# A transformer layer on one core: the low part of the FFN weights made by ScalarE and an accumulating transfer instead of VectorE

## The chip, the cores and the metric

The kernel runs on one core of one Trainium2 chip. The core has TensorE (PE in the profile; the loading of its stationary operand is shown apart as PEld), VectorE (DVE), ScalarE (ACT), GpSimd (POOL) and SyncE (SP), and 16 DMA engines that they share for transfers between DRAM and the on-chip memory. The queues from which transfers are issued are written SPq, ACTq and POOLq. The metric is the device time of one execution in microseconds; before the change it is 1370.73 us (median of three runs, 1368.98 to 1370.79). A measurement of this kernel can tell a difference of about 0.2% from no change.

## The reference, cut to what matters

The program computes one layer of a bidirectional encoder on 256 tokens of 2048 features, all in float32:

```python
h = rms_norm(x, g_mix)
proj = h @ w_in                       # 2048 x 8256: latents, rotary key, dilated q/k/v, gates
...                                   # latent attention -> y_a, dilated attention -> y_b
x = x + (g[:, :, 0] * y_a + g[:, :, 1] * y_b) @ w_o
gt, up = jnp.split(rms_norm(x, g_ffn) @ w_gate_up, 2, axis=-1)   # 2048 x 11264
return x + (jax.nn.silu(gt) * up) @ w_down                       # 5632 x 2048
```

The last two lines are the FFN. The change touches only how the weights `w_gate_up` and `w_down` are prepared.

## The kernel before

**Products.** Every weight matrix is cut into groups of at most 512 columns, and each group into blocks of two times 128 rows ("chunks" in the code): a block is a tile of 128 partitions by 2 x 512 float32, 512 KB. There are 481 blocks in all, in one fixed order: `w_in` with the small projections in between, the two attention outputs, `w_o`, and then the FFN. The FFN has 176 blocks of `w_gate_up` and 88 of `w_down`, 264 together, and it is the last stage of the program.

**Two parts for each operand.** TensorE multiplies in the format float32r. To keep float32 precision each operand is split in a high part (the value rounded to float32r) and a low part (what the rounding left). A product is then three matmuls, `mm3` (lines 384 to 386): high by high (L384), low weight by high activation (L385), high weight by low activation (L386). A block has two row slices, two halves of the tokens and three matmuls for each: 12 matmuls. The first row slice's L384 needs the high part `wh` alone; the next matmul, L385, needs the low part `wl`.

**The way of a block.** `load(i)` issues the transfer of block i from DRAM into a tile `w` from SyncE (L702). `split(i)` lets ScalarE copy `w` into `wh` (L710; the copy rounds) and VectorE subtract, `wl = w - wh` (L711). `products(i)` issues the 12 matmuls. The tiles `w`, `wh` and `wl` have four buffers each (`AHEAD + 1`).

**The order.** The order on every engine is the order in which the program is written; nothing is rearranged. At step i of the main loop it is: load of block i+4, split of block i+3, products of block i, then what takes a finished group out of the accumulators, and one piece of side work. So `wh` and `wl` of block i+3 take the buffers of block i-1, and can be written once the products of block i-1 are done; the products of block i+3 come three blocks later. The load of block i+4 takes the `w` buffer of block i, and can start once that block has been split.

**Beside it.** In the FFN, ScalarE also computes the SiLU of each gate group (L596) and VectorE multiplies it with the up group (L604); the result is transposed on TensorE (L201) and split in the same way into `hid0`, `hid1` (L171, L176). GpSimd has almost nothing to do: the factors of the norms (L160, L162), and at the start seven transfers of gain vectors (L124). The last thing the program does is to add the last group to the residual (L626) and to store it.

Of the kernel before, what the change touches and what calls it, by code (L numbers as in the profile page):

```python
# [14 lines left out]
AF = mybir.ActivationFunctionType  # L15
ALU = mybir.AluOpType
# [3 lines left out]
P = 128  # L20
S = 256
NT = S // P
# [59 lines left out]
def layer_kernel(ctx: ExitStack, tc: tile.TileContext, a: dict, out: bass.AP):  # L82
    nc = tc.nc
# [17 lines left out]
    def f32(ap):  # L101
        return ap.bitcast(F32)
# [4 lines left out]

# [1 line left out]
    ident = small([P, P], "ident")  # L109
# [38 lines left out]
    gains = Job(job_gains())  # L148
# [15 lines left out]

# [1 line left out]
    def split_evac(*parts):  # L166
        """each part: hi, lo, source and a factor per partition; all hi first, since hi and lo of a part may share tiles
        with the next one's."""
        for hi, lo, ps, scale in parts:
            if scale is None:  # L170
                nc.scalar.copy(hi, ps)  # L171
            else:
                nc.scalar.activation(hi, ps, AF.Copy, scale=scale)  # L173
        for hi, lo, ps, scale in parts:
            if scale is None:
                nc.vector.tensor_sub(lo, ps, f32(hi))  # L176
            else:
                nc.vector.scalar_tensor_tensor(lo, ps, scale, f32(hi), op0=ALU.mult, op1=ALU.subtract)  # L178

    class Act:  # L180
        """hi and lo parts of a transposed activation, in tiles of 4 blocks."""

# [13 lines left out]
    def transpose_in(act, k0, nk, src, gname=None):  # L196
        """blocks k0..k0+nk (nk <= 4, in one tile of act) from src(t, k) [tok, 128]."""
        ps = side(f"tr_{act.name}{k0}").rearrange("p (k s) -> p k s", s=S)
        for k in range(nk):
            for t in range(NT):  # L200
                nc.tensor.transpose(ps[:, k, t * P:(t + 1) * P], src(t, k0 + k), ident)  # L201
        h, l = act.tiles(k0 // 4)
        o = k0 % 4
        if gname is None:
            split_evac((h[:, o:o + nk], l[:, o:o + nk], ps[:, :nk], None))
        else:
            split_evac(*((h[:, o + k], l[:, o + k], ps[:, k], gain(gname, k0 + k)) for k in range(nk)))
# [29 lines left out]

# [1 line left out]
    cT, latjob = {"cq": Act("cqT", 4), "ckv": Act("ckvT", 4)}, {}  # L239
# [20 lines left out]

# [1 line left out]
    pb = {}  # L262
# [35 lines left out]

# [1 line left out]
    mla = {}  # L300
# [39 lines left out]
    def rope(x, A, B, nh, i):  # L340
        """x [P, NT, nh, 64] rotated in place, with the gain in the tables."""
        c = rt[:, 2 * i, :, None, :].to_broadcast([P, NT, nh, ROPE])
        s = rt[:, 2 * i + 1, :, None, :].to_broadcast([P, NT, nh, ROPE])
        nc.vector.tensor_mul(A, x, c)
        nc.vector.tensor_mul(B, x, s)
        h = ROPE // 2
        nc.vector.tensor_sub(x[..., :h], A[..., :h], B[..., h:])
        nc.vector.tensor_add(x[..., h:], B[..., :h], A[..., h:])
# [30 lines left out]

# [1 line left out]
    oT = {"mla": Act("oaT", H), "dil": Act("obT", H)}  # L381
# [6 lines left out]
    def job_attn(kind, p):  # L388
        h0 = 2 * p
        nm = f"{kind}{p}"  # L390
        if kind == "mla":
            qk, aux = mla["qk", p], mla["r", p]
            ss, v, r = (small([P, 12], f"{nm}{c}") for c in ("ss", "vv", "rr"))
# [16 lines left out]
            q, k = ([qk[:, c, t] for t in range(NT)] for c in range(2))  # L410
            g, sc = gqk_mla, MLA_SCALE
            vh, vl = ([mla["v", p][:, c, t] for t in range(NT)] for c in range(2))
        else:
            q, k = ([z.rearrange("p (h d) -> p h d", h=H)[:, h0:h0 + 2] for z in pb[n]] for n in ("qd", "kd"))
            vh, vl = ([pb["vd"][t][c].rearrange("p (h d) -> p h d", h=H)[:, h0:h0 + 2] for t in range(NT)]
                      for c in range(2))
            g = gqk_dil
        # transposes of q and k
        ps = side(nm + "qk").rearrange("p (c h s) -> p c h s", c=2, h=2)
# [19 lines left out]
        yield 1  # L439
        # scores  # L440
        ps = side(nm + "s").rearrange("p (h t s) -> p h t s", h=2, t=NT)
# [9 lines left out]
        if kind == "mla":  # L451
            src, esc = sv, sc
# [15 lines left out]
        yield 2  # L468
        # transposes of the probabilities
        ps = side(nm + "pt").rearrange("p (h c s) -> p h c s", h=2, c=2)  # L470
# [6 lines left out]
        yield 2  # L477
        # values
        ps = side(nm + "o").rearrange("p (h s) -> p h s", s=S)
# [7 lines left out]
    def job_prep_dil(n):  # L487
        """the norms of all heads: keys are scaled, the queries' factor waits for the scores"""
        z = [t.rearrange("p (h d) -> p h d", h=H) for t in pb[n]]
        ss = small([P, NT, H], "ss_" + n)  # L490
        for t in range(NT):
            sq = t4([P, H, 128], f"sq_{n}{t}")
            nc.scalar.activation(sq, z[t], AF.Square)
            nc.vector.tensor_reduce(ss[:, t], sq, axis=AX.X, op=ALU.add)
            yield 1
        r = rstd_of(ss, 128, "r_" + n)
        yield 2
        if n == "qd":
            st["rqd"] = small([P, NT, H], "rqd")
            nc.vector.tensor_scalar_mul(st["rqd"], r, DIL_SCALE)  # L500
        else:
            for t in range(NT):
                nc.vector.tensor_mul(z[t], z[t], r[:, t, :, None].to_broadcast([P, H, 128]))
                yield 1
# [7 lines left out]

# [1 line left out]
    g0, tj, mT, gbias = {}, {}, Act("mT", KD), {}  # L514
# [44 lines left out]

# [1 line left out]
    x1, hT, hjobs, xres = {}, Act("hT", KD), {}, {}  # L561
# [26 lines left out]

# [1 line left out]
    sg, hidT, djobs = {}, {}, {}  # L590
# [37 lines left out]

# [1 line left out]
    groups = []  # L630
# [34 lines left out]
    for j in range(4):  # L665
        groups.append(Group(W["w_o"], 512 * j, 512, range(KD), mT, evac_wo(j),
                            {k: (lambda k=k: [mjobs[k // 4]]) for k in range(KD)}))
    halves = (range(0, 6), range(6, 11))
    for half, js in enumerate(halves):
# [22 lines left out]
    early = {}  # L692

    def load(i):
        g, gi, ks, _, _ = chunks[i]
        if gi == 0 and i:
            load_x(ks[0] * P, (ks[-1] + 1) * P)
            if ks[-1] == KD - 1:
                load_rows()
        t = wp.tile([P, len(ks), g.n], F32, name=f"w{i}", tag="w")  # L700
        src = g.w[ks[0] * P:(ks[-1] + 1) * P, g.c0:g.c0 + g.n]
        nc.sync.dma_start(t, src.rearrange("(k p) n -> p k n", p=P))  # L702
        wt[i] = t

    def split(i):
        g, gi, ks, _, _ = chunks[i]
        t = wt.pop(i)
        h = wp.tile([P, len(ks), g.n], F32R, name=f"wh{i}", tag="wh")
        l = wp.tile([P, len(ks), g.n], F32R, name=f"wl{i}", tag="wl")
        nc.scalar.copy(h, t)  # L710
        nc.vector.tensor_sub(l, t, f32(h))  # L711
        parts[i] = (h, l)
# [110 lines left out]
def _tables():  # L823
    """Rotary angles, distances and how many patterns reach a key: constants of the shapes."""
    f = np.float32
# [30 lines left out]
```

## Time and profile before

The times are 1370.79, 1368.98 and 1370.73 us. The profiled execution has a span of 1367.5 us from the first to the last instruction; the median of the times is 3.2 us above this span, and these 3.2 us are taken as what lies around the span, since the profiled execution has no separate time beside it.

| what | before |
|---|---|
| median time | 1370.73 us |
| span of the profiled execution | 1367.5 us |
| TensorE busy in the span | 1356.5 us (99%) |
| VectorE busy | 758.1 us (55%) |
| ScalarE busy | 623.5 us (46%) |
| GpSimd busy | 32.3 us (2%) |
| data moved | 257.14 MB, mean 188 GB/s |
| first FFN product starts | 634.42 us |

How to read it: the busy time of TensorE counts overlapping matmuls once, and a busy TensorE is not TensorE at its peak. A row of a group of instructions gives the line, the engine, the operation, the tile written and the tiles read, the shape, the count, the busy time in us and the mean duration of one in ns, and then the idle time of the engine just before them and what ended it. A row of a window gives the stretch in us, the busy time of each engine in it, the TensorE clock that was granted, the share of the 16 DMA engines' time that was busy with packets, and the data rate. A timeline row gives the start and the duration in us.

### The profile page before, as it was taken

Reading aid. Unit: us, or ns where it says so; the run is one execution under the profiler, and the core shown is the slowest. Engines: PE = TensorE matmul, PEld = TensorE weight load, DVE = VectorE, ACT = ScalarE, POOL = GpSimd, SP = SyncE. Lnnn points to the kernel's source line nnn. Section 1 sums busy time; section 2 is a strip of 40 time slices with the busy share of each in tenths; the row PEclk is TensorE's granted clock in tenths of the full one; section 3 lists DMA queues with packets and bytes.
Section 4 is the critical chain, followed back from the end, with each engine's and each line's share of the span. In section 5 each row is a group of like instructions: output and inputs, shape, how many; then the busy total and the mean of one; then the engine's idle time right before and its main releaser. Section 6 shows DMA issues by size and latency. Waiting matters only on the chain.

```text
span 1367.5 us, 16361 instructions
## 1 busy us (share of the span) xinstructions
PE 1356.5 (99%) x6342; PEld 1144.7 (84%) x6342; DVE 758.1 (55%) x774; ACT 623.5 (46%) x776; POOL 32.3 (2%) x41
## 2 busy tenths in 40 slices
PE   7999999999999999999999999999999999999998
PEld 6899999888888888888888888888888888888887
DVE  5566777677655556555445544554444544555443
ACT  6555655454444444445444444433344444444332
POOL 1011111000000000000000000000000000000000
PEclk9999999999999999999999999999999999999999
DMA  8555555555566666565665665555665665565663
GB/s 259 175 173 168 158 172 177 174 166 172 178 202 199 198 190 216 193 210 181 196 192 182 191 198 184 187 189 193 194 193 187 194 197 188 186 188 183 202 212 123
DMA packets 138205, 257.14 MB, mean 188 GB/s; under 512 B 9192, under 2 KB 28688, under 8 KB 138128
## 3 DMA queue, kind: packets, MB, share of 16 engines
q1 hardware_dynamic: 137760, 255.96, 59.8%
q8 instruction: 49, 0.80, 0.2%
q14 instruction: 28, 0.23, 0.0%
q10 hardware_dynamic: 144, 0.13, 0.0%
q0 software_dynamic: 224, 0.01, 0.0%
HBM read 253.97 MB, written 2.10 MB: 187 GB/s over the span
## 4 chain that ended last, share of the span: by engine, by line
PE 99%; DMA 1%; SPq 0%; DVE 0%; issue 0%; ACT 0%; DVEq 0%
PE g L384 31%; PE g L386 31%; PE g L385 31%; PE tr_hid L201 1%; DMA w<-in_w_in_dram 1%; PE tr_hT L201 0%; PE tr_mT L201 0%; PE tr_xT L201 0%; DMA xn<-in_x_dram 0%; PE mla3s L386 0%; PE mla2s L386 0%; PE mla0s L386 0%; PE mla1s L386 0%; PE mla2s L385 0%; PE mla2s L384 0%; PE mla1s L385 0%
## 5 line engine op out<-in xcount | busy, mean ns | idle before, releaser
L711 DVE TENSOR_TENSOR wl<-w,wh 128x1024 fp32r<-128x1024 f32 (+2 forms) x481 | 575.6, 1201 | 472.8 <-ACT wh L710 470.8
L710 ACT CAST wh<-w 128x1024 fp32r<-128x1024 f32 (+2 forms) x481 | 496.2, 1036 | 537.6 <-PE g L386 489.7
L384 PE MATMUL g<-wh,hTh 128*128 128x512 f32 x704 | 274.8, 390 | 0.0
L386 PE MATMUL g<-wh,hTl 128*128 128x512 f32 x704 | 274.0, 389 | 0.0
L385 PE MATMUL g<-wl,hTh 128*128 128x512 f32 x704 | 273.9, 389 | 0.0
L384 PE MATMUL g<-wh,xTh 128*128 128x512 f32 (+1 forms) x544 | 210.2, 386 | 1.9 <-ACT xTh L173 1.9
L386 PE MATMUL g<-wh,xTl 128*128 128x512 f32 (+1 forms) x544 | 207.2, 381 | 0.5 <-DVE xTl L178 0.5
L385 PE MATMUL g<-wl,xTh 128*128 128x512 f32 (+1 forms) x544 | 207.2, 381 | 0.0
L386 PEld LDWEIGHTS g<-wh,hTl 128*128 128x128 f32 x704 | 132.1, 188 | 27.6
L385 PEld LDWEIGHTS g<-wl,hTh 128*128 128x128 f32 x704 | 132.2, 188 | 27.1
L384 PEld LDWEIGHTS g<-wh,hTh 128*128 128x128 f32 x704 | 132.2, 188 | 27.1
L384 PEld LDWEIGHTS g<-wh,xTh 128*128 128x128 f32 x544 | 102.7, 189 | 17.2 <-ACT xTh L173 2.1
L386 PEld LDWEIGHTS g<-wh,xTl 128*128 128x128 f32 x544 | 102.4, 188 | 17.3 <-DVE xTl L178 1.0
L385 PEld LDWEIGHTS g<-wl,xTh 128*128 128x128 f32 x544 | 102.6, 189 | 15.3 <-DVE wl L711 0.4
L384 PE MATMUL g<-wh,hid0h 128*128 128x512 f32 x192 | 74.8, 390 | 0.0
L386 PE MATMUL g<-wh,hid0l 128*128 128x512 f32 x192 | 74.7, 389 | 0.0
L385 PE MATMUL g<-wl,hid0h 128*128 128x512 f32 x192 | 74.7, 389 | 0.0
L384 PE MATMUL g<-wh,hid1h 128*128 128x512 f32 x160 | 62.3, 390 | 0.0
L386 PE MATMUL g<-wh,hid1l 128*128 128x512 f32 x160 | 62.2, 389 | 0.0
L385 PE MATMUL g<-wl,hid1h 128*128 128x512 f32 x160 | 62.2, 389 | 0.0
L384 PE MATMUL g<-wh,mTh 128*128 128x512 f32 x128 | 50.2, 392 | 0.0
L386 PE MATMUL g<-wh,mTl 128*128 128x512 f32 x128 | 49.8, 389 | 0.0
(509 smaller groups left out, 1233.5 us busy)
## 6 DMA issues: line engine op xcount, KB each, us to landing
w<-in_w_gate_up_dram SPq DMA_DIRECT2D x176, 512.0 KB, 4.5
w<-in_w_down_dram SPq DMA_DIRECT2D x88, 512.0 KB, 4.3
w<-in_w_in_dram SPq DMA_DIRECT2D x79, 512.0 KB, 4.2
w<-in_w_in_dram SPq DMA_DIRECT2D x56, 448.0 KB, 3.6
w<-in_w_o_dram SPq DMA_DIRECT2D x32, 512.0 KB, 4.5
w<-in_w_o_mla_dram SPq DMA_DIRECT2D x16, 512.0 KB, 4.1
w<-in_w_o_dil_dram SPq DMA_DIRECT2D x16, 512.0 KB, 4.2
w<-in_w_ukv_dram SPq DMA_DIRECT2D x8, 512.0 KB, 4.3
```

The costliest lines, as they stand in the source:

```text
L201: nc.tensor.transpose(ps[:, k, t * P:(t + 1) * P], src(t, k0 + k), ident)
L384: nc.tensor.matmul(ps, ah, bh, start=first, stop=False)
L385: nc.tensor.matmul(ps, ah, bl, start=False, stop=False)
L386: nc.tensor.matmul(ps, al, bh, start=False, stop=last)
L710: nc.scalar.copy(h, t)
L711: nc.vector.tensor_sub(l, t, f32(h))
```

## The change

For the blocks of the FFN (the groups from `ffn_at` on), `split` no longer lets VectorE subtract. ScalarE writes minus the high part into the tile of the low part (L718), and GpSimd issues a transfer of the same block of DRAM into that tile that adds what it brings to what lies there (L719): `wl = -wh + w`. The load of the block into `w` stays, since ScalarE makes the high part from it. For the blocks before the FFN nothing changes. The line numbers from there on shift by four to eight.

```diff
     for j in range(4):
         groups.append(Group(W["w_o"], 512 * j, 512, range(KD), mT, evac_wo(j),
                             {k: (lambda k=k: [mjobs[k // 4]]) for k in range(KD)}))
+    ffn_at = len(groups)
     halves = (range(0, 6), range(6, 11))
...
+    def source(i):
+        g, gi, ks, _, _ = chunks[i]
+        return g.w[ks[0] * P:(ks[-1] + 1) * P, g.c0:g.c0 + g.n].rearrange("(k p) n -> p k n", p=P)
+
     def load(i):
...
         t = wp.tile([P, len(ks), g.n], F32, name=f"w{i}", tag="w")
-        src = g.w[ks[0] * P:(ks[-1] + 1) * P, g.c0:g.c0 + g.n]
-        nc.sync.dma_start(t, src.rearrange("(k p) n -> p k n", p=P))
+        nc.sync.dma_start(t, source(i))
         wt[i] = t
 
     def split(i):
...
         nc.scalar.copy(h, t)
-        nc.vector.tensor_sub(l, t, f32(h))
+        if gi < ffn_at:
+            nc.vector.tensor_sub(l, t, f32(h))
+        else:
+            nc.scalar.activation(l, f32(h), AF.Copy, scale=-1.0)
+            nc.gpsimd.dma_start(l, source(i), accum_op=ALU.add)
         parts[i] = (h, l)
```

The order of the instructions on ScalarE, in the FFN around the first gate group's SiLU, with what each waits for in brackets (the names of the engines are those whose progress is waited for; DMAHW and DMASW are transfers issued by SyncE and by GpSimd). Before:

```order
L710 CAST wh_5389<-w_5369 128x1024 [waits DMAHW3_49,DVE_49,PE_49]
L710 CAST wh_5407<-w_5387 128x1024 [waits DMAHW4_49,DVE_49,PE_49]
L710 CAST wh_5425<-w_5405 128x1024 [waits DMAHW5_49,DVE_49,PE_49]
L710 CAST wh_5443<-w_5423 128x1024 [waits DMAHW6_49,DVE_49,PE_49]
L596 ACT_TABLE_LOAD [waits PE_49]
```

and in the changed kernel, at the same place:

```order
L714 CAST wh_5396<-w_5375 128x1024 [waits DMAHW3_49,PE_49]
L718 ACTIVATE wl_5397<-wh_5396 128x1024 [waits DMASW2_49,Activation_49]
L714 CAST wh_5415<-w_5394 128x1024 [waits DMAHW4_49,PE_49]
L718 ACTIVATE wl_5416<-wh_5415 128x1024 [waits DMASW3_49,Activation_49]
L714 CAST wh_5434<-w_5413 128x1024 [waits DMAHW5_49,PE_49]
L718 ACTIVATE wl_5435<-wh_5434 128x1024 [waits DMASW4_49,Activation_49]
L714 CAST wh_5453<-w_5432 128x1024 [waits DMAHW6_49,PE_49]
L718 ACTIVATE wl_5454<-wh_5453 128x1024 [waits DMASW5_49,Activation_49]
L596 ACT_TABLE_LOAD [waits PE_49]
```

After every copy to `wh` now stands the negated copy to `wl`; the wait of the copy on VectorE is gone.

The order on GpSimd, from the last norm factor of the attention to the factor of the FFN's norm. Before:

```order
L160 TENSOR_SCALAR r_kd_v<-ss_kd 128x16 [waits DVE_49]
L162 TENSOR_TENSOR r_kd<-r_kd_v,mhalf 128x16 [waits Pool_49]
L160 TENSOR_SCALAR r_v<-ss2s 128x2 [waits DVE_49]
L162 TENSOR_TENSOR r_5292<-r_v,mhalf 128x2 [waits Pool_49]
L852 UNCONDITIONAL_BRANCH
```

and in the changed kernel, at the same place:

```order
L162 TENSOR_TENSOR r_kd<-r_kd_v,mhalf 128x16 [waits Pool_49]
L719 DMA wl_5233<-in_w_gate_up_dram 128x2x512 [waits DVE_49,PE_49,Activation_49]
L719 DMA wl_5252<-in_w_gate_up_dram 128x2x512 [waits DVE_49,DMASW0_49,PE_49,Activation_49]
L719 DMA wl_5271<-in_w_gate_up_dram 128x2x512 [waits DVE_49,DMASW1_49,PE_49,Activation_49]
L160 TENSOR_SCALAR r_v<-ss2s 128x2 [waits DVE_49]
L162 TENSOR_TENSOR r_5295<-r_v,mhalf 128x2 [waits Pool_49]
L719 DMA wl_5301<-in_w_gate_up_dram 128x2x512 [waits DMASW2_49,PE_49,Activation_49]
L719 DMA wl_5321<-in_w_gate_up_dram 128x2x512 [waits DMASW3_49,DMASW7_49,PE_49,Activation_49]
```

GpSimd's queue now holds one transfer for each FFN block, three of them ahead of the norm's factor, and each waits for ScalarE's negated copy.

The order on TensorE at the first FFN block. Before:

```order
L384 MATMUL g_5301<-wh_5232,hTh_4826 128x512 [waits Activation_49]
L385 MATMUL g_5301<-wl_5233,hTh_4826 128x512 [waits DVE_49]
L386 MATMUL g_5301<-wh_5232,hTl_4827 128x512
L384 MATMUL g_5301<-wh_5232,hTh_4826 128x512
L385 MATMUL g_5301<-wl_5233,hTh_4826 128x512
```

and in the changed kernel:

```order
L384 MATMUL g_5305<-wh_5232,hTh_4826 128x512 [waits Activation_49]
L385 MATMUL g_5305<-wl_5233,hTh_4826 128x512 [waits DMASW7_49]
L386 MATMUL g_5305<-wh_5232,hTl_4827 128x512
L384 MATMUL g_5305<-wh_5232,hTh_4826 128x512
L385 MATMUL g_5305<-wl_5233,hTh_4826 128x512
```

The matmuls and their order are the same; the second of each block, the first that reads `wl`, waits for the transfer and no longer for VectorE.

## The prediction

> **What bounds the kernel now.** I read the first page's busy times and its chain first, then who kept TensorE waiting, and then the FFN alone.
>
> ```profile
> span 1367.5 us, 16361 instructions
> PE 1356.5 (99%) x6342; PEld 1144.7 (84%) x6342; DVE 758.1 (55%) x774; ACT 623.5 (46%) x776; POOL 32.3 (2%) x41
> PE 99%; DMA 1%; SPq 0%; DVE 0%; issue 0%; ACT 0%; DVEq 0%
> PE pg L135 <- DMA gmix_rows<-in_g_mix_dram: 2.4, 1, 2.4
> PE tr_xT L201 <- DMA xn<-in_x_dram: 2.1, 3, 0.9
> PE g L384 <- ACT xTh L173: 1.9, 1, 1.9
> PE g L386 <- DVE xTl L178: 0.5, 1, 0.5
> ```
>
> TensorE is the chain that ends last (99% of it), and the four wait rows are all it ever waited for: 2.4 + 2.1 + 1.9 + 0.5 = 6.9 us, all at the start. VectorE, at 55%, holds nothing up, so taking work from it can gain nothing by itself. What the change spends is ScalarE time, a longer way of each block to its low part, and transfers. The FFN shows how much of each is left:
>
> ```profile
> 634.42 0.39 PE L384 MATMUL g<-wh,hTh 128*128 128x512 f32 x1
> 1363.08 0.39 PE L386 MATMUL g<-wh,hid1l 128*128 128x512 f32 x1
> 626.46 1.05 ACT L710 CAST wh<-w 128x1024 fp32r<-128x1024 f32 x1 [1.67 <-PE g L386]
> 665.45 1.05 ACT L710 CAST wh<-w 128x1024 fp32r<-128x1024 f32 x1 [1.67 <-PE g L386]
> 668.17 1.05 ACT L710 CAST wh<-w 128x1024 fp32r<-128x1024 f32 x1 [1.67 <-PE g L386]
> w<-in_w_gate_up_dram SPq DMA_DIRECT2D x176, 512.0 KB, 4.5
> w<-in_w_down_dram SPq DMA_DIRECT2D x88, 512.0 KB, 4.3
> 634.00:1364.00 730.00, 729.47 (x3267) 604.71 (x3265) 358.65 (x311) 301.61 (x303) 0.89 (x2) 1.00 0.60 189
> ```
>
> The first two rows are the first and the last product of the FFN: it lasts from 634.42 to 1363.47. It has 176 + 88 = 264 blocks (the two load rows), so a block takes 729.05 / 264 = 2.76 us, transposes included; two copies to `wh` in a quiet place start 668.17 - 665.45 = 2.72 us apart, each released by TensorE after 1.67 us of idle time. The window row of the FFN has TensorE busy throughout, and the DMA engines at a share of 0.60 and 189 GB/s. So a block now has 2.72 us in which ScalarE and the DMA engines must do their part.
>
> **The change part by part.**
>
> *VectorE's subtraction goes.*
>
> ```profile
> L711 DVE TENSOR_TENSOR wl<-w,wh 128x1024 fp32r<-128x1024 f32 x415 | 506.6, 1224 | 457.0 <-ACT wh L710 455.7
> L710 ACT CAST wh<-w 128x1024 fp32r<-128x1024 f32 x415 | 436.1, 1054 | 511.7 <-PE g L386 465.3 <-DMA w<-in_w_down_dram 28.9 <-DMA w<-in_w_in_dram 10.9
> L536 ACT ACTIVATE g<-g x4: 1050/1051/1060, 377.7 to 497.8; 128x1024 f32<-128x1024 f32 x4
> ```
>
> 264 x 1.224 = 323 us of VectorE time vanish, from under TensorE: worth 0. It also frees `w` after the copy instead of after the subtraction, so loads can start about 1.2 us earlier; TensorE waits for none, so 0 again.
>
> *ScalarE's negated copy comes.* The nearest rows are the copy (1.054 us) and the activation of the same size (1.05 us). 264 x 1.05 = 277 us, and 2.1 us per block instead of 1.05: under 2.72 us, so ScalarE does not become the bound. Were it 1.5 us, the two would still fit.
>
> *The way of a block gets longer.* Copy, negated copy, GpSimd's issue, landing, then the second matmul. For GpSimd's issue and landing:
>
> ```profile
> L124 POOL DMA_DIRECT2D grow<-in_g_cq_dram x1: 717/717/717, 1.5 to 1.5; - x1
> L124 POOL DMA_DIRECT2D grow<-in_g_ffn_dram x1: 484/484/484, 4.7 to 4.7; - x1
> grow<-in_g_cq_dram POOLq DMA_DIRECT2D x1, 2.0 KB, 3.2
> grow<-in_g_ffn_dram POOLq DMA_DIRECT2D x1, 8.0 KB, 6.6
> DMA to landing us min/median/max: 2.8/4.3/8.4
> ```
>
> An issue took 0.48 to 0.72 us for 4 to 16 rows of a gain; the new one has 256 rows, which nothing here shows. The two rows show no growth with the rows; GpSimd would bind only at more than a block's time per issue, and I take 0.6 us. Landing, counted from the issue, is 4.3 us in the median for the weights' loads (last row) and at most 8.4. A buffer of `wl` goes round in 2.72 (products) + 0.1 + 1.05 + 1.05 + 0.6 + 4.3 = 9.8 us, and four buffers allow 4 x 2.72 = 10.9 us: by this alone the wait stays hidden by 1 us. With the longest landing, 8.4, it is 13.9 us, 3.48 per block. What queues behind a late transfer: on TensorE everything after the second matmul of the block, so the end itself; on GpSimd the later transfers; on ScalarE the next copies, because TensorE frees their buffers later.
>
> *The transfers: the term that decides.* Each block is fetched twice, and the second time something must also read what lies in `wl`. What can the engines carry?
>
> ```profile
> 8.00:12.00 4.00, 3.41 (x16) 2.45 (x14) 1.39 (x2) 1.05 (x1) 0.00 (x0) 1.00 1.05 373
> 12.00:16.00 4.00, 1.64 (x6) 1.07 (x7) 2.95 (x5) 3.29 (x6) 0.00 (x0) 1.00 1.07 375
> 16.00:20.00 4.00, 4.00 (x21) 3.30 (x20) 3.16 (x5) 3.68 (x9) 0.00 (x0) 1.00 1.07 374
> ```
>
> At the start, with several loads waiting at any time, three stretches in a row stand at 373, 375 and 374 GB/s with a DMA share above 1: that is saturation. A block of 524288 bytes costs 1.40 us there; I call it a unit. The other measure is the FFN's window: 524288 / 189 GB/s = 2.77 us, times the share 0.60, is 1.66 us. So a unit costs 1.40 to 1.66 us; I take 1.5, nearer the saturated rows, because there the engines moved data back to back, as they would have to now.
>
> How many units does an accumulating transfer cost? No row shows one. From below: 1 unit, if reading the old content runs beside the rest. From above: 3 units, if each engine reads the block, reads the old content and writes the sum one after the other. I take 2: a plain transfer reads a block and writes a block side by side, and here two blocks must be read for the one written. A block then costs 1 + 2 = 3 units = 4.5 us (4.21 to 4.98) against TensorE's 2.72, and the DMA engines become the bound. The ring of buffers does not: without the landing it takes 5.5 us, so four buffers at 4.5 us each leave a landing 12.5 us.
>
> The Trainium skill, "Collectives: The Full Stack", section "The bandwidth ceiling: the fold count and why AG ≠ RS ≠ AR", has the same reason for its reductions: two source reads go through one ring of each engine, and the rate it measured against a copy was lower by 1.93. By that figure the block would be 2.93 units, 4.40 us by my estimate, and the time some 26 us less than my sum; no run so far shows an accumulating transfer.
>
> **The sum.** The first FFN block's copy starts at 626.46; with 1.05 + 1.05 and 0.2 of signalling its transfer can start at 628.8. Then 264 x 4.5 = 1188 us of saturated transfers end at 1816.8. After the last landing come 2.6 us of its block's matmuls and 4.0 us from the last product to the end of the span (1367.5 - 1363.47): span 1823. The transposes, which make the 2.76 us per block out of 2.72, disappear in TensorE's waits. With the 3.2 us by which the median of the runs lies above the profiled span: **1827 us**, a third more than 1370.73. With 4.21 and 4.98 us per block it is 1750 and 1953.
>
> **The rivals.**
>
> *The old content is read for free: 2 units.* For it: reading the on-chip tile needs no DRAM, and DRAM may be what saturates at 374 GB/s. Against it: the same engines must still move it. The block costs 2.80 us at the saturated rate, up to 3.48 by the ring with the longest landing: 1378 to 1557, at 1.5 us per unit 1431.
>
> *Read, read and write in a row: 4 units or so.* For it: adding needs the old value before anything can be written, which a copy doesn't. Against it: many rows of 2 KB are in work at a time and could overlap. 4 x 1.5 = 6.0 us per block: 2223 (2120 to 2392).
>
> *One transfer at a time.* If GpSimd's preparation, or the engines, let no second accumulating transfer start before the first has landed, the price is a whole landing: at the longest seen, 8.4 us, 264 x 8.4 gives 2856. For it: the landings of the small gain transfers grew to 6.6 us beside the loads. Against it: seven of those were in flight at once.
>
> *TensorE slows down while it waits.*
>
> ```profile
> 6.97 0.63 PE L384 MATMUL g<-wh,xTh 128*128 128x512 f32 x1
> 7.40 0.63 PE L385 MATMUL g<-wl,xTh 128*128 128x512 f32 x1
> 10.15 0.39 PE L385 MATMUL g<-wl,xTh 128*128 128x512 f32 x1
> 10.38 0.40 PE L386 MATMUL g<-wh,xTl 128*128 128x512 f32 x1
> 0.00:10.00 10.00, 5.46 (x16) 3.64 (x17) 2.35 (x4) 3.53 (x6) 4.43 (x14) 1.00 0.69 208
> ```
>
> After the idle start matmuls come 0.43 us apart and later 0.23, though the clock column says 1.00 for that stretch. If the waits brought this back for good, a block is 12 x 0.43 = 5.16 us of TensorE and the FFN 264 x 5.16 = 1362: about 2004. At 4.5 us per block the gap is only 1.8 us, shorter than that at the start, and a slow TensorE has no gaps left to stay slow by. The Trainium skill, "TensorE: Matmul & The Clock Gate", section "What's actually happening", gives half the clock after one idle window of about 3.4 us; the early rows agree in the factor, and by that rule the gaps of my forecast would not close the gate, while those of the four-unit rival (3.3 us) nearly would.
>
> *Not slower.* The engines carry both transfers at one unit each in TensorE's time. That needs 1.049 MB in 2.76 us, 380 GB/s, 2% above the highest row, and landings below 5.4 us at full load. From that rate on nothing is left on the path: 1371, no change. A gain has no place to come from, with TensorE at 99%.
>
> *That the change does nothing* is excluded: the transfers stand in GpSimd's order, and TensorE waits for them.
>
> **How the numbers follow.** Three units 0.42; two units 0.17; four units 0.22; one at a time 0.10; slow TensorE 0.05; not slower 0.04; the forecast is the likeliest, 1827 us. The range reaches from the saturated two-unit time, 1378, to the top of the four units, 2392, rounded to 1380 and 2400; it leaves out one at a time and not slower, 0.14. The forecast's own range is 1750 to 1953. Differences under 0.2% cannot be told from no change: slower 0.96, within 0.2% 0.03, faster 0.01.
>
> **What would show it.** In the changed profile the FFN's windows should have a DMA share near 1.0, TensorE busy 60% of the time in bursts of 2.7 us, and the wait rows of TensorE headed by L385 for the transfer into `wl`, some 450 us in all (264 x 1.74). GpSimd's queue should carry 138 MB, and its packets twice the time per byte of the loads'. Everything before 626 us should stand as it is, and ScalarE gain 277 us. If the share in the FFN is clearly below 1 while TensorE waits, the bound is not the engines' work but a landing or GpSimd's issue, and the sum is wrong in kind; if the matmuls of the FFN are 0.43 us apart, it is the clock; a share near 1 at another time per block means a wrong number of units.

## The result and the profile after

The changed kernel takes 1705.45 us (median; 1703.09 to 1706.83) against 1369.86 us of the kernel before, measured beside it: 1.2449 times the time, 95% interval 1.2431 to 1.2466. The forecast was 1827 us, the range 1380 to 2400. The direction and the mechanism were right, the size of the loss was 336 us instead of 456: the time lies in the wide range, but below the 1750 to 1953 that the prediction gave as the forecast's own.

The first page of the changed kernel: span, busy times, queues and the chain that ended last.

```profile
span 1704.8 us, 16896 instructions
PE 1447.7 (85%) x6342; PEld 1138.0 (67%) x6342; DVE 437.7 (26%) x510; ACT 900.0 (53%) x1040; POOL 347.2 (20%) x305
q1 hardware_dynamic: 137760, 255.96, 45.9%
q0 software_dynamic: 72032, 138.44, 44.8%
DMA 49%; PE 46%; issue 5%; ACT 0%; POOL 0%; SPq 0%; DVE 0%; POOLq 0%; DVEq 0%
L718 ACT ACTIVATE wl<-wh 128x1024 fp32r<-128x1024 f32 x264 | 279.7, 1059 | 8.6
w<-in_w_gate_up_dram SPq DMA_DIRECT2D x176, 512.0 KB, 9.1
wl<-in_w_gate_up_dram POOLq DMA_DIRECT2D x176, 512.0 KB, 10.7
```

Before, TensorE was 99% of the chain; now half of it is transfers. VectorE lost 320 us and ScalarE gained 277 us, as the change says, and neither moved the end. GpSimd's queue (q0) carries 138 MB, the FFN weights a second time; over the whole execution its packets occupy the engines 1.8 times as long per byte as SyncE's (44.8% for 138.44 MB against 45.9% for 255.96 MB), where the prediction expected twice. A load of a block, which landed after 4.5 us, now takes 9.1, and the accumulating transfer 10.7.

Who kept TensorE waiting (line, tile, releaser; total, number and longest in us), GpSimd's issues, and the FFN's middle by the windows view:

```profile
PE g L385 <- DMA wl<-in_w_gate_up_dram: 162.5, 159, 4.1
PE g L385 <- DMA wl<-in_w_down_dram: 83.7, 71, 4.3
L719 POOL DMA_DIRECT2D wl<-in_w_gate_up_dram x176: 1180/1194/1295, 629.1 to 1523.7; - x176
700.00:1500.00 800.00, 613.60 (x2475) 444.22 (x2476) 31.24 (x34) 438.45 (x427) 237.68 (x200) 1.00 1.09 262
1600.00:1690.00 90.00, 69.00 (x262) 51.29 (x261) 2.45 (x2) 44.91 (x43) 25.05 (x21) 0.92 1.07 253
```

All the new waits stand at L385, the first matmul of a block that reads `wl`, and their releaser is the transfer into `wl`. They come to 246 us, not to the 450 of the prediction; together with the 91 us by which TensorE's busy time grew (1356.5 to 1447.7 us) they are the 337 us by which the span grew. TensorE is busy for 77% of the FFN's middle, where 60% was expected. In the middle of the FFN the DMA share is 1.09 where it was 0.60, and the rate 262 GB/s. Two blocks of 524288 bytes at 262 GB/s are 4.00 us: that is the new time of a block, and the timeline shows it directly, the second matmul of four successive blocks:

```profile
999.99 0.50 PE L385 MATMUL g<-wl,hTh 128*128 128x512 f32 x1 [0.96 <-DMA wl<-in_w_gate_up_dram]
1003.98 0.50 PE L385 MATMUL g<-wl,hTh 128*128 128x512 f32 x1 [0.93 <-DMA wl<-in_w_gate_up_dram]
1008.03 0.50 PE L385 MATMUL g<-wl,hTh 128*128 128x512 f32 x1 [1.03 <-DMA wl<-in_w_gate_up_dram]
1011.99 0.50 PE L385 MATMUL g<-wl,hTh 128*128 128x512 f32 x1 [0.90 <-DMA wl<-in_w_gate_up_dram]
```

Four microseconds a block, of which TensorE works three and waits one. What these pages cannot tell apart: four buffers of `wl` at 4.00 us each are also exactly a round of 16 us, so either the engines are full, or the ring of buffers with its long landing sets the pace and the landing is the cause, not the consequence.

### The profile page after: what moved, and what is told of

Its sections match the earlier page's. It is cut to its first block, busy times and chain, and to the rows that moved or that the text cites. A ratio compares the mean times of both kernels' runs of the same rounds, so it can differ in the third digit from the quotient of the medians.

```text
span 1704.8 us, 16896 instructions
## 1 busy us (share of the span) xinstructions
PE 1447.7 (85%) x6342; PEld 1138.0 (67%) x6342; DVE 437.7 (26%) x510; ACT 900.0 (53%) x1040; POOL 347.2 (20%) x305
## 3 DMA queue, kind: packets, MB, share of 16 engines
q1 hardware_dynamic: 137760, 255.96, 45.9%
q0 software_dynamic: 72032, 138.44, 44.8%
## 4 chain that ended last, share of the span: by engine, by line
DMA 49%; PE 46%; issue 5%; ACT 0%; POOL 0%; SPq 0%; DVE 0%; POOLq 0%; DVEq 0%
DMA wl<-in_w_gate_up_dram 32%; DMA wl<-in_w_down_dram 16%; PE g L385 15%; PE g L386 14%; PE g L384 13%; DMA w<-in_w_in_dram 1%; POOL wl L719 0%; PE tr_mT L201 0%; PE tr_xT L201 0%; DMA xn<-in_x_dram 0%; PE tr_hT L201 0%; ACT wl L718 0%; ACT wh L714 0%; PE mla3s L386 0%; PE mla1s L386 0%
## 5 line engine op out<-in xcount | busy, mean ns | idle before, releaser
L385 PE MATMUL g<-wl,hTh 128*128 128x512 f32 x704 | 297.4, 422 | 163.0 <-DMA wl<-in_w_gate_up_dram 162.5
L719 POOL DMA_DIRECT2D wl<-in_w_gate_up_dram x176 | 210.0, 1193 | 891.1 <-ACT wl L718 452.6
L385 PEld LDWEIGHTS g<-wl,hTh 128*128 128x128 f32 x704 | 133.7, 190 | 256.6 <-DMA wl<-in_w_gate_up_dram 233.3
L716 DVE TENSOR_TENSOR wl<-w,wh 128x1024 fp32r<-128x1024 f32 (+2 forms) x217 | 252.9, 1173 | 141.2 <-ACT wh L714 140.2
L718 ACT ACTIVATE wl<-wh 128x1024 fp32r<-128x1024 f32 x264 | 279.7, 1059 | 8.6
L385 PE MATMUL g<-wl,xTh 128*128 128x512 f32 (+1 forms) x544 | 207.8, 382 | 0.0
L604 DVE SCALAR_TENSOR_TENSOR sg<-g,r,sg 128x512 f32<-128x512 f32 x22 | 15.5, 746 | 591.9 <-PE g L386 591.9
L719 POOL DMA_DIRECT2D wl<-in_w_down_dram x88 | 104.9, 1192 | 256.2 <-ACT wl L718 243.1
L385 PE MATMUL g<-wl,hid0h 128*128 128x512 f32 x192 | 80.5, 420 | 47.2 <-DMA wl<-in_w_down_dram 47.0
L385 PEld LDWEIGHTS g<-wl,xTh 128*128 128x128 f32 x544 | 102.9, 189 | 15.4 <-DVE wl L716 0.4
L385 PE MATMUL g<-wl,hid1h 128*128 128x512 f32 x160 | 69.6, 435 | 36.9 <-DMA wl<-in_w_down_dram 36.7
L385 PEld LDWEIGHTS g<-wl,hid0h 128*128 128x128 f32 x192 | 36.0, 187 | 73.5 <-DMA wl<-in_w_down_dram 67.3
L617 DVE TENSOR_TENSOR x<-g,x 128x1024 f32<-128x1024 f32 x7 | 8.6, 1225 | 289.4 <-PE g L386 289.4
## 6 DMA issues: line engine op xcount, KB each, us to landing
wl<-in_w_gate_up_dram POOLq DMA_DIRECT2D x176, 512.0 KB, 10.7
wl<-in_w_down_dram POOLq DMA_DIRECT2D x88, 512.0 KB, 10.7
```

Of the source, the lines that this page charges most:

```text
L385: nc.tensor.matmul(ps, ah, bl, start=False, stop=False)
L604: nc.vector.scalar_tensor_tensor(z[:, t], ps[:, t], st["2"][:, t:t + 1], z[:, t], op0=ALU.mult, op1=ALU.mult)
L617: nc.vector.tensor_add(x1[j], ps, x1[j])
L718: nc.scalar.activation(l, f32(h), AF.Copy, scale=-1.0)
L719: nc.gpsimd.dma_start(l, source(i), accum_op=ALU.add)
```

## The experiments

In what follows, a block's time is worked out as (time - 649) / 264, where 649 is the profiled span of the changed kernel less 264 times 4.00 us; where a window's rate is quoted, it is the bytes of a block's transfers over that rate.

### Is it the ring or the engines?

First, the same kernel with a longer ring. The edit:

```diff
-AHEAD = 3
+AHEAD = 5
...
-    tp = ctx.enter_context(tc.tile_pool(name="tp", bufs=34))
+    tp = ctx.enter_context(tc.tile_pool(name="tp", bufs=28))
```

> The changed kernel with blocks prepared five ahead instead of three (six buffers for w, wh and wl instead of four; the pool of other tiles has 28 buffers instead of 34 to make room). In the changed kernel a buffer's round takes 4 x 4.02 = 16.1 us. If the engines' work is the bound, the period stays 4.02 us and the landing only grows from 10.7 to some 18 us: 1705 us, within 1%. If the ring of buffers is the bound, 16.1 us over six buffers is 2.7 us and TensorE binds: about 1371 us.

Measured: 1697.33 us, 1.2392 times before (1.2374 to 1.2411). The landing and the windows of this kernel:

```profile
wl<-in_w_gate_up_dram POOLq DMA_DIRECT2D x176, 512.0 KB, 18.7
700.00:1500.00 800.00, 611.44 (x2471) 442.08 (x2470) 31.24 (x34) 438.24 (x426) 237.81 (x200) 1.00 1.10 262
```

Two buffers more gave the same 262 GB/s and 8.0 us more of landing, which is two block times: the transfers only stand longer in the queue. The engines are the bound and the landing is the consequence.

The longer lead has a price of its own, so the kernel before was run with the same two edits as a control.

> The kernel before with blocks prepared five ahead (six buffers each, 28 instead of 34 in the other pool), as a control for the runs that have this: 1370 us, within 0.3%. If the smaller pool or the longer lead costs something by itself, that much has to be taken off those runs.

It took 1375.82 us, 1.0044 times before (1.0029 to 1.0059), and not the 1370 expected; in the profiled executions the FFN starts 4.7 us later than before (639.10 against 634.42 us), and 3.5 us of this is one wait at the start, for the first activations behind more splits, which was 1.9 us before:

```profile
PE g L384 <- ACT xTh L173: 5.4, 1, 5.4
```

So of the runs with six buffers some 6 us are the control's. Against it, the changed kernel gained 8 + 6 = 14 us from the longer ring. Block by block the two traces differ at the FFN's two ends. The first product of the thirteenth block comes 54.5 us after that of the first with four buffers, and 43.9 us with six, which have two more blocks under way when the FFN starts. From there to the last two dozen blocks the two keep nearly one pace (six buffers are 7.6 us ahead at the 237th block), and over those the lead grows to 15.3 us: there the four buffers ran at 253 GB/s and a clock of 0.92 (the window of 1600 to 1690 us above). The clock falls near the end with six buffers as well (0.85 from 1600 to 1650 us), and what starts the late landings there is not shown.

### What does an accumulating transfer cost the engines?

The kernel without the FFN's loads: `w` is one block that stays, and per block only the accumulating transfer is left. (Since `wl` is `w - wh` for whatever `wh` is, the two parts still sum to the weight; only the low part is no longer small.)

```diff
+    fix = []
+
     def load(i):
         g, gi, ks, _, _ = chunks[i]
+        if gi >= ffn_at:
+            if not fix:
+                fix.append(wp.tile([P, CK, 512], F32, name="wfix", tag="w"))
+                nc.sync.dma_start(fix[0], source(i))
+            wt[i] = fix[0]
+            return
```

> The changed kernel without the loads of the FFN blocks into w: the high parts are all made from one block that stays (the output is therefore not the layer's). What is left per block is one accumulating transfer. Engines' work at two units for it: 2.7 us, TensorE binds, 1371 to 1390 us. If the accumulating transfer by itself is as slow as a block's period (an addition unit that runs at 130 GB/s, or one at a time), about 1705 us.

Measured: 1430.92 us, between the two expectations. The window of its FFN:

```profile
700.00:1400.00 700.00, 674.97 (x2911) 532.87 (x2910) 34.91 (x37) 516.71 (x502) 281.38 (x236) 1.00 1.05 179
```

And the same with each accumulating transfer issued twice, the second time into one of three scratch tiles:

```diff
+            for k in range(3 - len(xs)):
+                xs.append(wp.tile([P, CK, 512], F32, name=f"xs{k}", tag="w"))
+                nc.gpsimd.memset(xs[k], 0.0)
             nc.gpsimd.dma_start(l, source(i), accum_op=ALU.add)
+            nc.gpsimd.dma_start(xs[i % 3], source(i), accum_op=ALU.add)
```

> As the kernel without FFN loads, and each block's accumulating transfer is issued a second time, into one of three scratch tiles: two accumulating transfers per block and no plain one, so that the engines and not TensorE set the pace and the price can be read (the output is not the layer's). Engines' work at two units of 1.34 us each: 5.36 us per block, 644 + 264 x 5.36 = 2059 us. At 1.93 plain loads of 1.40 us each it is 5.41 us, 2072. If an accumulating transfer costs three units, 8.0 us per block and 2760 us; if one unit, 2.7 us and about 1380 us. The ring alone, with a landing that stays near 10.7 us, would leave 4.0 us and 1705 us.

Measured: 1990.97 us, 68 us below the nearer of the two-unit expectations, since 5.08 us a block are less than the 5.36 put in. The windows of this kernel:

```profile
700.00:1500.00 800.00, 591.74 (x1938) 427.18 (x1939) 23.34 (x25) 343.90 (x335) 377.12 (x315) 0.84 1.13 206
```

206 GB/s at a share of 1.13, in each 100 us from 700 to 1800: an accumulating transfer of one block takes the saturated engines 524288 / 206 GB/s = **2.55 us**. That is under TensorE's 2.76, so the engines cannot be what held the kernel without loads at 1431 us.

To compare, three plain transfers per block: GpSimd's second one overwrites, and SyncE fetches the block a third time into a tile that nobody reads.

```diff
-            nc.gpsimd.dma_start(l, source(i), accum_op=ALU.add)
+            nc.gpsimd.dma_start(l, source(i))
+            x = wp.tile([P, len(ks), g.n], F32, name=f"wx{i}", tag="wx")
+            nc.sync.dma_start(x, source(i))
```

> As the kernel whose second transfer overwrites, and SyncE fetches the block a third time, into a scratch tile that nothing reads: three plain transfers per FFN block and no addition (the pool of other tiles has 30 buffers for it; the output is not the layer's). If an accumulating transfer is nothing but one more block to be read (two accumulating ones per block took 5.10 us, so 2.55 each), three plain ones should take the engines nearly what a load and an accumulating one take: 3 x 1.40 = 4.2 us by the saturated rate, 1750 us; 1700 to 1760. If the addition itself is what is slow and plain transfers are cheaper than 1.40 when many are queued, clearly less, down to 3 x 1.2 = 3.6 us and 1600 us.

Measured: 1718.93 us, 1.2542 times before (1.2517 to 1.2567), beside 1.2449 of the changed kernel. Its windows:

```profile
700.00:1500.00 800.00, 618.12 (x2435) 455.05 (x2434) 31.25 (x34) 432.45 (x420) 140.31 (x197) 0.97 1.12 387
```

387 GB/s in each 100 us from 700 to 1500, with the clock anywhere from 0.94 to 1.00: a plain block takes 1.355 us, three take 4.06. A load and an accumulating transfer take 4.00. So one accumulating transfer costs about what two plain ones do: 2.55 / 1.355 = 1.88 of them by the kernel with two per block, (4.00 - 1.355) / 1.355 = 1.95 by the changed kernel. The same kernel shows that the extra block need not come with an addition: a third fetch does the same damage. And it shows that DRAM is not what is full in the changed kernel, where it gives 262 GB/s: here it gives 387. What these runs price is the transfer as a whole; whether the engines spend the second unit on reading the old content or on the addition itself, no run separates.

Does the extra read cost as much when it is of an on-chip tile, as the accumulating transfer's is? The third transfer now copies the high part from its tile:

```diff
-            nc.sync.dma_start(x, source(i))
+            nc.sync.dma_start(x, f32(h))
```

> As the kernel with three plain transfers, but the third copies the block's high part from its on-chip tile to the scratch tile: DRAM gives two blocks, the engines read three. If the engines' reading is the limit, wherever from, 4.0 to 4.2 us per block again, 1700 to 1760 us. If what saturates at 374 GB/s is DRAM and a read of an on-chip tile is nearly free, 2.8 us per block by the transfers, and then the ring of four buffers as in the kernel whose second transfer overwrites: about 1500 us.

Measured: 1783.76 us, slower than with the third fetch from DRAM. Its windows:

```profile
700.00:1500.00 800.00, 595.45 (x2316) 440.56 (x2314) 28.61 (x31) 410.74 (x400) 133.46 (x187) 0.95 1.09 368
```

Not 1500 but more than 1718, above both expectations: a copy from an on-chip tile is not free for the engines. In its best 100 us (700 to 800) the three blocks move at 382 GB/s with a share of 1.12, nearly as three loads do; in its worst (1100 to 1200) at 351, with a share of 1.05 and a clock of 0.91. The 368 are the mean of such stretches. That speaks for gaps rather than for a dearer copy; but the copy also holds the buffer of `wh` until it has landed and stands in SyncE's queue ahead of later loads, and no run with more buffers was made to separate this.

### Where two plain transfers lose

The one edit that takes only the addition away:

```diff
-            nc.gpsimd.dma_start(l, source(i), accum_op=ALU.add)
+            nc.gpsimd.dma_start(l, source(i))
```

> The same kernel, but GpSimd's second transfer of each FFN block overwrites the low part's tile instead of adding to it (the low part is therefore the whole weight, so the output is not the layer's). Issue, queue, size and rows are the same; only the addition is gone. Engines' work (the accumulating transfer costs two units of about 1.34 us because it reads two blocks): two units per block, 2.7 to 2.8 us against TensorE's 2.76, so 1371 to 1390 us. Rival, GpSimd's software queue or its destination type is what is slow, whatever the operation: about 1705 us. Rival, the ring of four buffers with its landing: the landing falls to that of two plain transfers, 5 to 8 us, so 1371 to 1450 us.

Measured: 1507.75 us, 1.0978 times before (1.0923 to 1.1032): some 120 us over what two units would give, and above the 1450 that the ring was given. The issue, the landings of GpSimd's transfers (minimum, median, maximum), who kept TensorE waiting, and the windows:

```profile
L719 POOL DMA_DIRECT2D wl<-in_w_gate_up_dram x176: 713/716/795, 630.2 to 1357.4; - x176
DMA to landing us min/median/max: 4.0/6.4/9.9
PE g L385 <- DMA wl<-in_w_gate_up_dram: 58.2, 25, 4.2
PE g L385 <- DMA wl<-in_w_down_dram: 32.7, 20, 4.0
700.00:1400.00 700.00, 633.61 (x2660) 506.94 (x2659) 32.46 (x35) 472.11 (x461) 153.95 (x215) 0.96 1.01 321
```

The rate, 321 GB/s, is below the 373 to 387 the engines can carry, so they are not the bound, though their share is 1.01; 45 waits of 2 us each in the mean are, and after several of them TensorE's clock fell (0.96 in the mean). Two causes were open, the ring and GpSimd's queue. The same kernel with six buffers:

> The kernel whose second transfer overwrites took 1507.75 us, not the 1371 to 1390 that two units give. Two causes are open. The ring: landing there is 6.4 us in the median and 9.9 at most, with 5.5 us for the rest that is more than 4 x 2.72 = 10.9. Or GpSimd's queue moves plain rows slower than SyncE's. Here blocks are prepared five ahead (six buffers). If the ring is the cause, only the two units are left: 2.8 us per block, 1371 to 1390 us. If the queue is, the time stays near 1500 us.

Measured: 1383.75 us, 1.0099 (1.0080 to 1.0118); its windows:

```profile
1000.00:1100.00 100.00, 100.00 (x447) 82.91 (x446) 5.08 (x5) 78.51 (x76) 25.93 (x37) 1.00 1.18 382
```

Here TensorE is busy throughout with both transfers beside it, at 382 GB/s and with the highest share of all, 1.18; from 700 to 1300 us the mean is 377 GB/s, and TensorE never waits. Of the 8 us over the control, 6.0 are five waits for transfers of `w_down` near the end. So it was the ring: with four buffers 2.72 us of products, 2.5 from release to issue and a landing of 6.4 make 11.6 us, more than the 10.9 that four blocks allow; that arithmetic alone gives 2.9 us a block where 3.25 were measured, and I put the rest down to late landings and the falling clock. And for the kernel without loads:

> The kernel without FFN loads took 1430.92 us though an accumulating transfer takes the engines 2.55 us by the kernel with two of them per block. If the ring of four buffers is the cause (landing 6.1 us), six buffers bring it to TensorE's pace: 1371 to 1380 us. If the engines need more than 2.76 us for one accumulating transfer per block, it stays at about 1430 us.

Measured: 1375.11 us, 1.0034 (1.0021 to 1.0047), the control's own time; no wait at L385 is left. One accumulating transfer per block, at 2.55 us, hides entirely under TensorE once the ring is long enough. Its window of the FFN:

```profile
700.00:1300.00 600.00, 600.00 (x2689) 497.72 (x2688) 32.47 (x35) 477.38 (x465) 258.81 (x217) 1.00 1.09 191
```

The share is 1.09, as in the changed kernel, and 1.05 with four buffers, where TensorE did wait: the share does not say whether the engines are the bound.

### Half as many, and ScalarE alone

Only every second FFN block accumulates; the others are split by VectorE.

```diff
-        if gi < ffn_at:
+        if gi < ffn_at or i % 2:
```

> The changed kernel, but only every second FFN block gets its low part by the negated copy and the accumulating transfer; the others by VectorE as before. Engines: per pair of blocks two loads at 1.40 and one accumulating transfer at 2.55 us are 5.35, 2.68 per block, under TensorE's 2.76. If the engines' work were the only bound, 1371 to 1375 us. With the ring as well: an accumulated buffer's round is 2.72 + 2.8 for release, copies and issue + a landing of 6 to 7, some 12 us, in four blocks 3.0 us each: about 1435 us (1400 to 1460).

Measured: 1542.55 us, 1.1276 (1.1233 to 1.1319): worse than either expectation. The landing, and the windows:

```profile
wl<-in_w_gate_up_dram POOLq DMA_DIRECT2D x88, 512.0 KB, 7.4
700.00:1400.00 700.00, 615.99 (x2555) 484.37 (x2554) 157.40 (x137) 344.78 (x340) 124.00 (x104) 0.96 0.91 233
```

The rate, 233 GB/s, is below the 282 that the same mix reaches with six buffers (next run, 700 to 1300 us), so it is the ring again, with a longer landing (7.4 against the 6 to 7 I put in) and a clock of 0.96 that stretches the products within each round: 2.72 + 2.5 + 7.4 = 12.6 us over four buffers is 3.2 us a block, and the measured (1542.55 - 649) / 264 is 3.4; the rest I put down to the clock and to landings above the median, without a run that separates them. With six buffers:

> The same with blocks prepared five ahead (six buffers each, 28 instead of 34 in the other pool): the ring allows 16.3 us, more than the 12 needed, and the engines need 2.68 us per block. Both terms together give TensorE's pace, 1371 to 1378 us. If halving the accumulating transfers leaves a cost of its own (GpSimd's issue, interference with the loads), clearly more, 1385 us and up.

Measured: 1382.33 us, 1.0093 (1.0078 to 1.0108): 6.5 us over the control, of which three waits for transfers of `w_down` are 4.7; the engines' sum of 2.68 us per block is close under TensorE's 2.76. That misses the expected 1371 to 1378, which left out the control's 6 us, and with them holds at its upper end.

Last, ScalarE's part alone: the negated copy, then VectorE's addition in place of the transfer.

```diff
-            nc.gpsimd.dma_start(l, source(i), accum_op=ALU.add)
+            nc.vector.tensor_add(l, t, f32(l))
```

> ScalarE's negated copy alone: wl gets minus wh by ScalarE, and VectorE adds w to it in place of the transfer. It adds 264 x 1.06 = 280 us of ScalarE work and one more hand-over between the engines, no transfer. If ScalarE's part costs nothing, 1371 us, within 0.3% of before. If the longer chain counts (copy, copy, addition: 1.05 + 1.06 + 1.22 us and hand-overs against 8.2 us of lead), still nothing, as 3.6 is under 8.2. A loss over 5 us would mean that ScalarE's queue holds up what it takes out of the accumulators.

Measured: 1371.41 us, 1.0016 (1.0007 to 1.0025), and ScalarE's busy time as in the changed kernel:

```profile
PE 1358.6 (99%) x6342; PEld 1145.4 (84%) x6342; DVE 759.3 (55%) x774; ACT 898.6 (66%) x1040; POOL 32.3 (2%) x41
```

The 275 us of ScalarE cost some 2 us (1 to 3.4 by the interval). None of these versions could have beaten the kernel before: TensorE is its chain at 99%, and none of the edits takes work from TensorE.

## Why the prediction was right

**The bound moves from TensorE to the DMA engines: right.** The waits are at L385 for the transfer into `wl`, and two more buffers change nothing in the rate, 262 GB/s. The share near 1 that the prediction named as the sign (1.09 here) is no proof by itself, as the kernels without loads show.

**VectorE's relief is worth 0, ScalarE's copy costs 0: right.** 320 us went from VectorE and nothing came of it; the copy took 1.059 us (I took 1.05), and its run alone lost 2 us.

**An accumulating transfer is two units: right.** 1.88 and 1.95 by two different runs. This is what carried the forecast; the range, 1380 to 2400, would have held with two or with four units as well. The rival that the old content is read for free falls with the 2.55 us; the rival of four units would have needed three for the accumulating one, 4.07 us; the rival of one at a time falls with the kernel with two per block, which finishes one every 2.55 us, while the shortest landing of an accumulating transfer in the kernels without loads is 5.5 us. The Trainium skill's reason in "Collectives: The Full Stack", section "The bandwidth ceiling: the fold count and why AG ≠ RS ≠ AR", is two source reads, with a ratio of 1.93; the ratio agrees with these traces, 1.88 to 1.95, while the second read itself is not seen in them.

**The unit is the term that was mis-sized.** I took 1.5 us, between 1.40 of the saturated rows and 1.66 from the FFN's window. Measured is 1.355 in the kernel with three plain transfers, and 4.00 / 3 = 1.33 over the changed kernel's block: below even my lower bound. The upper bound was no bound at all: it scaled the FFN's window to a share of 1, though the saturated rows stood at 1.05 to 1.07 and the new ones at 1.09 to 1.13, and though the share for each GB/s was higher in the unhurried FFN (0.60 / 189 = 0.0032) than in the saturated rows (1.07 / 375 = 0.0029). The sum with 4.00 is 628.8 + 1056 + 9.8 = 1695 us; about the 11 us to 1705 are what six buffers took away at the FFN's start and end.

**The ring: argued with too little slack.** I called it hidden by 1 us with a median landing of 4.3 us, and used it only for the two-unit rival. In the changed kernel six buffers were worth some 14 us. But that rival's own time, 1431, was wrong for it: with the addition taken away the kernel ran at 1508, inside the bounds I gave (1378 to 1557) and set by the ring, not by 2 x 1.5 us. Two things were late there: GpSimd's issue takes 0.72 us for a plain block and 1.19 for an accumulating one, not 0.6, and two transfers side by side land later than one. The rival of "not slower" asked for 380 GB/s, which is 1% above the highest row and not 2%, and in this part it was right: two plain transfers do fit under TensorE, at 377 GB/s in the mean, with six buffers. It had the accumulating transfer at one unit, and that was wrong.

**Slow TensorE: right to leave it out, for this kernel.** In the FFN's middle the clock column stays at 1.00, with gaps of about 1 us; near the FFN's start and end, where single waits reach 4 us, it stands at 0.90 to 0.93, and the mean of the whole execution is 0.989.

## What to carry to other kernels

An accumulating transfer into on-chip memory moves one block, and cost the DMA engines about two here: count it twice, add everything else that is in flight, and compare with the saturated rate of this kernel's own trace before moving an addition from a compute engine to a transfer. Moving work off an engine that isn't on the chain gains nothing, and its new place must be shown to have room, in throughput and in latency apart. The share of the DMA engines does not tell the two apart: it stood at 1.01 and 1.05 in two kernels that the ring of buffers held back, and at 1.18 where TensorE did not wait. The rate against the saturated rate of the same mix tells more, and more buffers answer it: if the rate stays and the landing grows by whole block times, it is throughput; if the waits go, it was the ring.

## What the runs showed of the hardware that was not expected

- An issue from GpSimd has the same length for every block but depends on the operation: 0.716 us for a plain transfer of 256 rows of 2 KB, 1.194 us for an accumulating one, against 0.48 to 0.72 for a few short rows.
- TensorE's clock fell after shorter waits than I had allowed for. In the kernel with two accumulating transfers per block the clock column stands at 0.84; this stretch of its timeline shows a matmul after a wait of 2.06 us, the next ones 0.23 us apart, and from a microsecond later on 0.43:

```profile
1008.27 0.50 PE L385 MATMUL g<-wl,hTh 128*128 128x512 f32 x1 [2.06 <-DMA wl<-in_w_gate_up_dram]
1008.61 0.39 PE L386 MATMUL g<-wh,hTl 128*128 128x512 f32 x1
1008.84 0.40 PE L384 MATMUL g<-wh,hTh 128*128 128x512 f32 x1
1009.08 0.47 PE L385 MATMUL g<-wl,hTh 128*128 128x512 f32 x1
1009.34 0.63 PE L386 MATMUL g<-wh,hTl 128*128 128x512 f32 x1
1009.77 0.63 PE L384 MATMUL g<-wh,hTh 128*128 128x512 f32 x1
1010.20 0.63 PE L385 MATMUL g<-wl,hTh 128*128 128x512 f32 x1
```

  The Trainium skill, "TensorE: Matmul & The Clock Gate", section "What's actually happening", speaks of one idle window of about 3.4 us; here waits of about 2 us were often enough. Counted over the FFN of this kernel's timeline, 99 of the 120 waits for a transfer of 2.0 to 2.25 us are followed within a few matmuls by the spacing of 0.43 us, and none of the 115 shorter than 1.75 us; in the changed kernel none of 219 such short waits is. Why the others near 2 us are not followed is not shown.
- The saturated rate is not one number: 373 to 375 GB/s at the start of the kernel before, 387 with three plain transfers per block. What makes the difference these runs do not show.
